# A hybrid RG-LRU and mLSTM decoder step: when the rows of w_out are loaded, the order of the mLSTM output products, and the load of W

## The chip, the cores and the metric

One core of one Trainium2 chip runs the whole program. Its engines are TensorE (PE; PEld is its weight load), VectorE (DVE), ScalarE (ACT), GpSimd (POOL) and SyncE (SP), which here only issues DMAs; GpSimd issues DMAs too. The metric is the device time of one execution in microseconds. Lower is better.

## The reference

One layer of a decoder runs on a prompt of 1,024 tokens and, apart from it, on eight decode tokens that bring their own state. The core of what must be computed:

```python
hn = rmsnorm(x, g_norm)
u = hn @ w_in                                  # 1024 -> 7 x 1024 + 8 columns
xa, za, uq, uk, uv, uo, zb, ui, uf = split(u)
yA, hA, bufA = rglru_branch(xa, ...)           # causal conv, two gates, linear scan
hB, C, n, m = mlstm_seq(q, k, v, ig, lf, ...)  # 4 heads of 256, chunks of 128 tokens
yB = sigmoid(uo) * hB
yB = yB * rsqrt(mean(yB * yB, per head) + EPS) * g_mhead
merged = concat([yA * silu(za), yB * silu(zb)])   # 2048 wide
x = x + merged @ w_out                            # (2048, 1024)
y = rmsnorm(x, g_final)
```

Within a chunk, with `w = exp(D - m_t)` the masked decay weights, each head computes

```python
P = w * einsum('bthk,bshk->bhts', q, k)
num = einsum('bhts,bshv->bthv', P, v) + ginter * einsum('bthk,bhkv->bthv', q, C)
C_new = carry_scale * C + einsum('bhs,bshk,bshv->bhkv', decay, k, v)
```

The program returns y for prompt and decode tokens and the states of both branches.

## The kernel before

The large products are made from operands split into a high and a low part: `split` copies the value into a rounded type on ScalarE, and VectorE subtracts to get the rest; `mm3` then adds three products (high x high, high x low, low x high; lines 64 to 66).

**The input projection** walks over 14 units (`UNITS`) of two 256-column blocks of `w_in`. Each unit takes seven products, `Q_P1` to `Q_P4`, whose left operands (`cb_hi`, `cb_lo`, one pair for each of the seven) are made once from the normalised prompt and lie in 14 slots `b0` to `b13` of the pool `bpool`: `cb_hi` of product q in slot 2q, `cb_lo` in slot 2q+1. The last unit is the last reader of these slots, so product by product they become free there. The other operands, `wh` and `wl`, are split two products ahead into the pool `ws`, six slots of 4 KB a partition, from two raw tiles (`raw0`, `raw1`, 8 KB a partition each).

Between the halves of the products, `pop_bg` emits background work from queues: gates, RG-LRU, decode, the first chunk of the mLSTM (`m_first`), and, in the last unit, rows 0 to 7 of `w_out`.

**w_out** has 16 row blocks of 128 x 1024. `wo_load(n)` asks for rows n and n+1, each into a `ws` slot (`oraw`, line 1180). `wo_prep(n)` multiplies both with the decode tokens' merged activations (line 1194; `mAd` for rows 0 to 7, `mBd` for 8 to 15, both 32 columns wide with eight in use; the sums stay in the PSUM bank `tr` over all 16 rows) and splits them: rows 0 to 7 plainly into slot m, rows 8 to 15 with the head gain `gm4` multiplied in (lines 1203 and 1204), rows 14 and 15 into the raw slots. `wo_due(q)`, called after product q of the last unit, queues `wo_prep(0)`, `(2)`, `(4)`, `(6)` and, after the last product, the load of the first RG-LRU rows (`o_load(0)`). Rows 8 to 11 are prepared before the chunk loop, 12 and 13 in item 4, 14 and 15 in item 5.

**The chunk loop** runs over items n = 4 to 31: chunk c = n // 4, head h = n % 4. For each item `m_a` makes scores and weights, `m_b` the output and the new state, `m_g` and `m_z` gate, normalise and transpose the output into `mh`, `ml`. `m_load(n + 2)` fetches W, q and k, and v two items ahead. W is the row of decay exponents, broadcast to 128 partitions (three buffers); `m_k` adds a bias and the mask on VectorE (line 1038), takes the exponential on ScalarE (line 1039), and `m_a` multiplies the scores with it (line 1067).

Between these steps `fill` emits pieces of the output projection, two row blocks each, from the generators in `work`. `out_part(c, half, part)` makes one half (512 columns) of one tile of 128 tokens; part 0 uses the eight RG-LRU row blocks, part 1 the eight mLSTM row blocks, both into one PSUM tile (`o`, three banks). After part 1 the tile is added to x on VectorE (line 1275), squared on ScalarE (line 1276), and after both halves normalised by `finish`. A chunk's share of `work` is: part 0 of half 0 of tile c, part 1 of both halves of tile c-1, part 0 of half 1 of tile c. The last tile is made apart by `last_part` and `last_tile`.

What decides the order: the code gives the instructions in program order with symbolic buffers, and a planner in the build orders each engine's queue ahead of time. It takes, at each moment of its own model of the run, the earliest instruction in program order that is ready by that model; so an instruction that is ready early can stand far ahead of its place in the code, and a load can stand as early as its buffer is free. On the chip each queue runs strictly in that order.

## Time and profile before

| | |
|---|---|
| Median of 3 runs | 966.44 us (966.21 to 969.55) |
| The profiled execution | 970.22 us, of which span 968.1 us |
| Mean granted TensorE clock | 0.993 |
| TensorE busy | 941.3 us (97%) |
| VectorE, ScalarE, GpSimd busy | 697.4, 546.1, 146.5 us |
| Moved by DMA | 153.17 MB, mean 158 GB/s |

The busy time of an engine in a window says whether it is full there; the clock beside it says how fast TensorE was allowed to run. Successive large matmuls start 0.23 us apart and are listed with 0.39 us each, since they overlap; so short waits can hide in a "busy" TensorE, and the starts are what counts. In timelines, the bracket behind an instruction is the idle time of its engine just before it, and what ended it. "issue" of a DMA is the instruction on the queue; the landing is seen in the wait of who uses the data.

### The profile page before, as it was taken

What the parts mean: (1) busy time and instruction counts of PE and PEld (TensorE: products, weight loads), DVE (VectorE), ACT (ScalarE), POOL (GpSimd) and SP (SyncE); (2) the same over time, 40 slices, a digit from 0 to 9 for tenths busy, and PEclk for the clock granted to TensorE, in tenths of its full rate; (3) what the DMA queues carried; (4) which work ended last, traced back from release to release, by engine and by line L of the source; (5) the groups of instructions that cost most, each with busy time, mean ns of one, the idle gap of its engine ahead of it and who ended that gap; (6) DMA issues with size and microseconds to landing.
All of it is one profiled execution on the core that took longest, in us unless ns stands there. A gap on an engine that the chain in (4) does not pass through costs nothing.

```text
span 968.1 us, 15367 instructions
## 1 busy us (share of the span) xinstructions
PE 941.3 (97%) x5402; PEld 768.4 (79%) x5402; DVE 697.4 (72%) x1447; ACT 546.1 (56%) x984; POOL 146.5 (15%) x260
## 2 busy tenths in 40 slices
PE   7999989999999999899999999999999999999997
PEld 7797767777787988687889898875667788888886
DVE  6775898988888877777786846686566677676764
ACT  6554456666666756454566744456546366465643
POOL 1111112121212122202212221010200100000020
PEclk9999999999999999999999999999999999999999
DMA  5431447356645455437645453424973754564481
GB/s 191 137 126 43 131 134 271 129 176 196 220 152 196 166 177 172 156 124 242 193 163 167 150 180 95 157 93 154 308 212 98 197 142 128 150 184 140 120 110 49
DMA packets 129314, 153.17 MB, mean 158 GB/s; under 512 B 13750, under 2 KB 107990, under 8 KB 129230
## 3 DMA queue, kind: packets, MB, share of 16 engines
q1 hardware_dynamic: 111510, 96.33, 33.8%
q0 software_dynamic: 17728, 55.87, 16.7%
q8 instruction: 42, 0.69, 0.3%
q14 instruction: 34, 0.28, 0.1%
HBM read 100.59 MB, written 51.65 MB: 157 GB/s over the span
## 4 chain that ended last, share of the span: by engine, by line
PE 43%; DMA 5%; DVE 5%; issue 4%; ACT 1%; POOL 0%; SPq 0%; DVEq 0%; POOLq 0%; ACTq 0%
PE ps_o L66 7%; PE ps_o L64 7%; PE ps_o L65 7%; PE ps_kv L64 5%; PE ps_kv L65 5%; PE ps_kv L66 5%; DMA W<-d_alpha 3%; PE ps_tr L227 1%; PE ps_s L1058 1%; DVE Cl L71 1%; PE ps_qp L64 1%; DVE Cf L1119 1%; DMA rh<-d_rm 1%; PE ps_qp L65 1%; PE ps_qp L66 1%
## 5 line engine op out<-in xcount | busy, mean ns | idle before, releaser
L70 ACT CAST wh<-raw 128x1024 fp32r<-128x1024 f32 x91 | 95.5, 1050 | 74.7 <-PE ps_o L65 24.5
L71 DVE TENSOR_TENSOR wl<-raw,wh 128x1024 fp32r<-128x1024 f32 x91 | 110.9, 1218 | 31.6 <-ACT wh L70 19.4
L64 PE MATMUL ps_kv<-cb_hi,wh 128*128 128x512 f32 x320 | 129.0, 403 | 0.1
L66 PE MATMUL ps_kv<-cb_hi,wl 128*128 128x512 f32 x320 | 126.1, 394 | 0.0
L65 PE MATMUL ps_kv<-cb_lo,wh 128*128 128x512 f32 x320 | 125.9, 393 | 0.0
L64 PE MATMUL ps_o<-cb_hi,wh 128*128 128x512 f32 x240 | 94.7, 394 | 0.0
L66 PE MATMUL ps_o<-cb_hi,wl 128*128 128x512 f32 x240 | 93.9, 391 | 0.0
L65 PE MATMUL ps_o<-cb_lo,wh 128*128 128x512 f32 x240 | 93.7, 390 | 0.0
L64 PEld LDWEIGHTS ps_kv<-cb_hi,wh 128*128 128x128 f32 x320 | 60.4, 189 | 24.8 <-issue 5.5
L66 PEld LDWEIGHTS ps_kv<-cb_hi,wl 128*128 128x128 f32 x320 | 60.5, 189 | 15.7 <-issue 2.5
L65 PEld LDWEIGHTS ps_kv<-cb_lo,wh 128*128 128x128 f32 x320 | 60.6, 189 | 11.9
L66 PE MATMUL ps_o<-wo,ml 128*128 128x512 f32 (+1 forms) x136 | 52.2, 384 | 3.2 <-DVE ml L71 3.1
L64 PE MATMUL ps_kv<-wh,cb_hi 128*128 128x256 f32 x192 | 55.3, 288 | 0.0
L65 PE MATMUL ps_kv<-wl,cb_hi 128*128 128x256 f32 x192 | 54.3, 283 | 0.0
L66 PE MATMUL ps_kv<-wh,cb_lo 128*128 128x256 f32 x192 | 54.3, 283 | 0.0
L64 PE MATMUL ps_o<-wo,rh 128*128 128x512 f32 (+1 forms) x136 | 53.9, 397 | 0.0
L64 PEld LDWEIGHTS ps_o<-cb_hi,wh 128*128 128x128 f32 x240 | 45.1, 188 | 10.8 <-issue 1.7
L66 PEld LDWEIGHTS ps_o<-cb_hi,wl 128*128 128x128 f32 x240 | 45.0, 188 | 10.3 <-issue 0.8
L64 PE MATMUL ps_o<-wo,mh 128*128 128x512 f32 (+1 forms) x136 | 52.9, 389 | 0.0
L65 PE MATMUL ps_o<-wo,rh 128*128 128x512 f32 (+1 forms) x136 | 52.3, 384 | 0.0
L65 PEld LDWEIGHTS ps_o<-cb_lo,wh 128*128 128x128 f32 x240 | 45.1, 188 | 9.0
L66 PE MATMUL ps_o<-wo,rl 128*128 128x512 f32 (+1 forms) x136 | 52.1, 383 | 0.0
(469 smaller groups left out, 2506.9 us busy)
## 6 DMA issues: line engine op xcount, KB each, us to landing
raw<-in_w_in_dram SPq DMA_DIRECT2D x56, 512.0 KB
Cb<-in_state_mlstm_C_dram SPq DMA_DIRECT2D x32, 256.0 KB
out_dram<-Cb POOLq DMA_DIRECT2D x32, 256.0 KB, 4.6
qk<-d_qk SPq DMA_DIRECT2D x32, 256.0 KB
oraw<-in_w_out_dram SPq DMA_DIRECT2D x16, 512.0 KB
d_qk<-s POOLq DMA_DIRECT2D x24, 256.0 KB, 4.2
x<-in_x_prompt_dram SPq DMA_DIRECT2D x8, 512.0 KB
d_x<-s POOLq DMA_DIRECT2D x16, 256.0 KB, 2.9
```

Source lines behind the costliest of these rows:

```text
L64: TE.matmul(out, ah, bh, start=first, stop=False, skip_group_check=True)
L65: TE.matmul(out, ah, bl, start=False, stop=False, skip_group_check=True)
L66: TE.matmul(out, al, bh, start=False, stop=last, skip_group_check=True)
L70: A.copy(hi, src)
L71: V.tensor_tensor(lo, src, hi.bitcast(F32), op=ALU.subtract)
L227: TE.matmul(pz[32 * g:32 * g + 32, :], hnd[:, k, :], raws[u, k // 4][:, k % 4, :], start=k < 4, stop=k >= 4, skip_group_check=True)
L1058: TE.matmul(S, qk[:, 2 + kb, :], qk[:, kb, :], start=kb == 0, stop=kb == 1)
L1119: V.scalar_tensor_tensor(mx["Cf"][h][:, kb, :], mx["Cf"][h][:, kb, :], cs_b[:, h, c:c + 1], kvs[kb], op0=ALU.mult, op1=ALU.add)
```

## The change

Three parts, and small ones with them.

1. `wo_load` puts rows 0 to 7 as pairs into one operand slot, `b1`, rows 8 and 9 into `raw0`, rows 10 and 11 into `raw1`, and only rows 12 to 15 into `ws` slots. The split rows go to other slots (`WO_SLOT`): row 0 to `b0`, rows 1 to 12 to `b2` to `b13`, row 13 to `b1`. `wo_load` is called ahead of `wo_prep`, which now splits a single row and, for an even row, first issues the decode products of the pair (`wo_dec`). In the last unit rows 0 to 11 are due instead of 0 to 7; rows 12 and 13 come before the chunk loop, 14 in item 4, 15 in item 5. `o_load(0)` is called after the fifth product instead of the seventh.
2. Part 1 of a tile is one generator, `out_m(c)`: the first pair of heads (row blocks 8 to 11) for both halves, then the second pair (12 to 15) for both halves. Part 0 is `out_r(c, half)`. The order in `work` stays.
3. W has four buffers, and `m_load(n)` calls `w_load(n + 1)`: q, k and v are asked for two items ahead as before, W three.

With them: the decode weights are 32 columns wide for rows 0 and 1 only (`mA0`), which write all 32 rows of each sum once, and eight columns wide for all others, so the clearing of `mBd` on GpSimd goes, and one VectorE step in `rg_final` becomes two.

```diff
-    mAd = const([P, 8, 32], "mAd")
+    mA0, mA1 = const([P, 2, 32], "mA0"), const([P, 6, NB], "mA1")
...
-        V.scalar_tensor_tensor(mAd[:, :, 0:NB], OC[:, :, 4:12], 0.5, na, op0=ALU.mult, op1=ALU.mult)
+        for d, s in ((mA0[:, :, 0:NB], slice(0, 2)), (mA1, slice(2, 8))):
+            V.scalar_tensor_tensor(d, OC[:, s, 4:12], 0.5, na[:, s], op0=ALU.mult, op1=ALU.mult)
...
-        mB.append(sg([P, 8, 32], "mBd"))
+        mB.append(sg([P, 8, NB], "mBd"))
         mBd = mB[0]
-        G.memset(mBd, 0.0)
...
+        w_load(0)
         m_load(0)
         m_load(1)
...
-        W = mx["p"].tile([P, L], F32, tag="W", name="W", bufs=3)
-        ld(W, d_alpha[h:h + 1, ts_].rearrange("o t -> (o t)").partition_broadcast(P))
+        w_load(n + 1)
...
+    def w_load(n):
+        if n < 4 * NCH:
+            c, h = n // 4, n % 4
+            Ws[n] = mx["p"].tile([P, L], F32, tag="W", name="W", bufs=4)
+            ld(Ws[n], d_alpha[h:h + 1, c * L:(c + 1) * L].rearrange("o t -> (o t)").partition_broadcast(P))
...
+    WO_SLOT = [0, 2, 3, 4, 5, 6, 7, 8, 9, 10, 11, 12, 13, 1, 14, 15]
+
+    def wo_buf(slot, name, dt=F32R):
+        return big(slot, [P, 2, T], name, dt) if slot < 14 else rawp.tile([P, 2, T], dt, tag=f"raw{slot - 14}", name=name)
+
     def wo_load(n):
 
-        for m in (n, n + 1):
-            oraw[m] = ws([P, T], f"oraw{m}", F32)
-            ld(oraw[m], w_out[0, m * P:(m + 1) * P, :])
-
-    def wo_prep(n):
+        if n < 12:
+            t = wo_buf({8: 14, 10: 15}.get(n, 1), f"oraw{n}", F32)
+            rows = [t[:, 0], t[:, 1]]
+        else:
+            rows = [ws([P, T], f"oraw{n + i}", F32) for i in range(2)]
+        for i, r in enumerate(rows):
+            ld(r, w_out[0, (n + i) * P:(n + i + 1) * P, :])
+            oraw[n + i] = r
+
+    def wo_dec(n):
...
+                TE.matmul(dec_o[0][32 * g:32 * g + (32 if n == 0 else NB), :], md, oraw[m][:, half * 512:(half + 1) * 512],
+                          start=n == 0, stop=n == 14, skip_group_check=True)
+
+    def wo_prep(m):
+
+        if m % 2 == 0:
+            wo_dec(m)
+        raw = oraw.pop(m)
+        t = wo[m] = wo_buf(WO_SLOT[m], f"wo{m}")
+        if m < 8:
+            split(t[:, 0], t[:, 1], raw)
+        else:
+            gm = gm4[:, m - 8:m - 7]
+            A.mul(t[:, 0], raw, gm)
+            V.scalar_tensor_tensor(t[:, 1], raw, gm, t[:, 0].bitcast(F32), op0=ALU.mult, op1=ALU.subtract)
...
+    def out_m(c):
+
+        x = ot[c]
+        for pair in range(2):
+            for half in range(2):
+                yield from out_mm(x, half, (ch[c]["mh"], ch[c]["ml"]), 1, range(4 * pair, 4 * pair + 4))
+                if pair == 0:
+                    continue
...
+                V.tensor_tensor(x["y"][half], x["y"][half], x["p", half], op=ALU.add)
+                A.activation(x["p", half], x["y"][half], AF.Square, accum_out=x["ms"][:, half:half + 1])
...
     def wo_due(q):
 
+        if q > 0:
+            wo_prep(2 * q - 1)
         if q < 4:
+            wo_load(2 * q)
+        if q == 4:
+            wo_load(8)
+            wo_load(10)
+            o_load(0)
+        if q == 5:
+            wo_load(12)
+        if q < 6:
             bg.append(lambda: wo_prep(2 * q))
-        if q == 6:
-            bg.append(lambda: o_load(0))
...
-    work.extend([out_part(0, 0, 0), out_part(0, 1, 0), out_part(1, 0, 0), out_part(0, 0, 1), out_part(0, 1, 1),
-                 out_part(1, 1, 0)])
+    work.extend([out_r(0, 0), out_r(0, 1), out_r(1, 0), out_m(0), out_r(1, 1)])
     m_k(4)
-    wo_load(8)
+    wo_prep(12)
+    wo_load(14)
     fill(2)
-    wo_load(10)
-    wo_prep(8)
+    wo_prep(13)
     fill(2)
-    wo_load(12)
-    wo_prep(10)
...
             if c == 1:
-                wo_prep(12)
-                wo_load(14)
+                wo_prep(14)
                 o_load(1)
...
             if c == 1:
-                wo_prep(14)
+                wo_prep(15)
```

More of the change, by code (lines that the diff above doesn't have):

```diff
@@ L141, in hymba_kernel @@
     dEM = dconst([P, NB, NH], "dEM")
-    mAd = const([P, 8, 32], "mAd")
+    mA0, mA1 = const([P, 2, 32], "mA0"), const([P, 6, NB], "mA1")
     hnd = dconst([P, KC, 32], "hnd")
-    for t in (mAd, hnd):
+    for t in (mA0, hnd):
         G.memset(t, 0.0)
@@ L960, in decode_outputs @@
         for kb in range(2):
-            V.tensor_tensor(v4(mBd[:, :, 0:NB], kb), v4(num, kb), rsq, op=ALU.mult)
+            V.tensor_tensor(v4(mBd, kb), v4(num, kb), rsq, op=ALU.mult)
         yield
@@ L1015, in m_load @@
         ld(vt, d_v[h][ts_, :])
-        it[n] = {"qk": qk, "vt": vt, "W": W}
+        it[n] = {"qk": qk, "vt": vt}
+    Ws = {}
+    def w_load(n):
[3 more added lines that the diff above has]
+            ld(Ws[n], d_alpha[h:h + 1, c * L:(c + 1) * L].rearrange("o t -> (o t)").partition_broadcast(P))
     sos = {}
@@ L1036, in m_k @@
         d = it[n]
-        W = d["W"]
+        W = d["W"] = Ws.pop(n)
         V.scalar_tensor_tensor(W, W, be_t[:, c, h:h + 1], maskT, op0=ALU.add, op1=ALU.min)
@@ L1168, in m_z @@
         split(x["mh"][:, s, :], x["ml"][:, s, :], z)
-    wo = []
+    wo = {}
     dec_o = []
     oraw = {}
+    WO_SLOT = [0, 2, 3, 4, 5, 6, 7, 8, 9, 10, 11, 12, 13, 1, 14, 15]
+    def wo_buf(slot, name, dt=F32R):
+        return big(slot, [P, 2, T], name, dt) if slot < 14 else rawp.tile([P, 2, T], dt, tag=f"raw{slot - 14}", name=name)
     def wo_load(n):
-        for m in (n, n + 1):
-            oraw[m] = ws([P, T], f"oraw{m}", F32)
-            ld(oraw[m], w_out[0, m * P:(m + 1) * P, :])
@@ L1182, in wo_prep @@
-    def wo_prep(n):
+        if n < 12:
[7 more added lines that the diff above has]
+    def wo_dec(n):
         if n == 0:
             dec_o.append(ps("tr", [P, 512]))
-        if n not in oraw:
-            wo_load(n)
@@ L1189, in wo_prep @@
         for i in range(2):
             m = n + i
-            md = mAd[:, m, :] if m < 8 else mB[0][:, m - 8, :]
+            md = mA0[:, m, :] if m < 2 else mA1[:, m - 2, :] if m < 8 else mB[0][:, m - 8, :]
             for half in range(2):
                 g = 2 * i + half
-                TE.matmul(dec_o[0][32 * g:32 * g + 32, :], md, oraw[m][:, half * 512:(half + 1) * 512], start=n == 0,
-                          stop=n == 14, skip_group_check=True)
-        for m in (n, n + 1):
-            raw = oraw.pop(m)
-            t = big(m, [P, 2, T], f"wo{m}") if m < 14 else rawp.tile([P, 2, T], F32R, tag=f"raw{m - 14}", name=f"wo{m}")
-            if m < 8:
-                split(t[:, 0], t[:, 1], raw)
-            else:
-                gm = gm4[:, m - 8:m - 7]
-                A.mul(t[:, 0], raw, gm)
-                V.scalar_tensor_tensor(t[:, 1], raw, gm, t[:, 0].bitcast(F32), op0=ALU.mult, op1=ALU.subtract)
-            wo.append(t)
+                TE.matmul(dec_o[0][32 * g:32 * g + (32 if n == 0 else NB), :], md, oraw[m][:, half * 512:(half + 1) * 512],
+                          start=n == 0, stop=n == 14, skip_group_check=True)
@@ L1255, in o_load, with out_r, out_mm @@
         ot[c] = {"r": (mh, ml)}
-    def out_part(c, half, part):
+    def out_r(c, half):
         x = ot[c]
-        if part == 0:
-            x["p", half] = ps("o", [P, 512])
-        mh, ml = x["r"] if part == 0 else (ch[c]["mh"], ch[c]["ml"])
+        x["p", half] = ps("o", [P, 512])
+        yield from out_mm(x, half, x["r"], 0, range(8))
+    def out_mm(x, half, mhl, part, ks):
+        mh, ml = mhl
         hs = slice(half * HT, (half + 1) * HT)
-        for k in range(8):
+        for k in ks:
             w = wo[8 * part + k]
@@ L1268, in out_part @@
                 yield
-        if part == 1:
-            if half == 0:
-                x["ms"] = fms()
-                x["y"] = [sg([P, HT], f"y{n}") for n in range(2)]
-                for n in range(2):
-                    stq(x["y"][n], x_prompt[0, c * P:(c + 1) * P, n * HT:(n + 1) * HT])
-            V.tensor_tensor(x["y"][half], x["y"][half], x["p", half], op=ALU.add)
-            A.activation(x["p", half], x["y"][half], AF.Square, accum_out=x["ms"][:, half:half + 1])
-            if half == 1:
-                finish(P, x["y"], x["ms"], y_p[0, c * P:(c + 1) * P, :], True)
-                del ot[c], ch[c]
+    def out_m(c):
[5 more added lines that the diff above has]
+                    continue
+                if half == 0:
+                    x["ms"] = fms()
+                    x["y"] = [sg([P, HT], f"y{n}") for n in range(2)]
+                    for n in range(2):
+                        stq(x["y"][n], x_prompt[0, c * P:(c + 1) * P, n * HT:(n + 1) * HT])
+                V.tensor_tensor(x["y"][half], x["y"][half], x["p", half], op=ALU.add)
+                A.activation(x["p", half], x["y"][half], AF.Square, accum_out=x["ms"][:, half:half + 1])
+        finish(P, x["y"], x["ms"], y_p[0, c * P:(c + 1) * P, :], True)
+        del ot[c], ch[c]
     LP = [slice(0, 512), slice(512, 768), slice(768, 1024)]
@@ L1418, in hymba_kernel @@
         if h == 0 and c > 1:
-            work.extend([out_part(c, 0, 0), out_part(c - 1, 0, 1), out_part(c - 1, 1, 1)])
-            work.append(out_part(c, 1, 0) if c < last else last_part(0))
+            work.extend([out_r(c, 0), out_m(c - 1), out_r(c, 1) if c < last else last_part(0)])
         m_a(n)
```

## The prediction

> **What bounds the kernel now.** I read the page first, then the busy time by stage, then TensorE's waits, then the timelines around the places where TensorE stands still.

> ```profile
> span 968.1 us, 15367 instructions
> ## 1 busy us (share of the span) xinstructions
> PE 941.3 (97%) x5402; PEld 768.4 (79%) x5402; DVE 697.4 (72%) x1447; ACT 546.1 (56%) x984; POOL 146.5 (15%) x260
> ```

> TensorE is busy for 97% of the span, and the change takes no product away. It can win only where TensorE idles, runs at a lower clock, or issues small matmuls badly. By stage (the last two rows are parts of the second):

> ```profile
> core 0: us, PE busy (x) PEld busy (x) DVE busy (x) ACT busy (x) POOL busy (x), PEclk, DMA share, GB/s
> 640.00:690.00 50.00, 49.83 (x217) 33.30 (x216) 33.38 (x65) 26.31 (x35) 5.09 (x11) 1.00 0.53 173
> 690.00:725.00 35.00, 32.87 (x163) 21.90 (x162) 22.21 (x40) 17.69 (x32) 3.54 (x7) 0.95 0.77 247
> 725.00:770.00 45.00, 43.15 (x236) 34.81 (x235) 29.23 (x92) 23.05 (x63) 4.87 (x9) 1.00 0.52 150
> 700.00:710.00 10.00, 8.18 (x44) 5.82 (x43) 6.32 (x11) 5.84 (x10) 0.00 (x0) 0.94 1.03 317
> 710.00:720.00 10.00, 10.00 (x49) 6.54 (x47) 6.06 (x16) 4.32 (x11) 0.55 (x1) 0.89 0.36 105
> ```

> 640 to 690 is the last unit of the input projection, with the first eight rows of w_out between its products; 690 to 725 is the passage to the chunk loop, with the other eight. The unit is full. The passage idles 2.1 us, has the lower clock, and there the DMA engines are full (1.03). What stands still in it, on TensorE, ScalarE and the load queue:

> ```profile
> 706.02 0.39 PE L66 MATMUL ps_o<-wo,rl 128*128 128x512 f32 x1
> 708.23 0.39 PE L64 MATMUL ps_qp<-vh,ph 128*128 128x258 f32 x1 [1.82 <-ACT hh L1114]
> ...
> 700.08 0.93 SPq L1180 DMA_DIRECT2D oraw<-in_w_out_dram  x2
> ...
> 705.83 1.15 ACT L1203 ACTIVATE wo<-oraw,gm 128x1024 fp32r<-128x1024 f32 x1 [3.52 <-DMA oraw<-in_w_out_dram]
> ...
> 707.71 0.47 ACT L1114 ACTIVATE hh<-ps_qp,gi_t 128x257 f32<-128x257 f32 x1
> ```

> The chain: row 14 is requested at 700.08 and lands at 705.83. ScalarE stands in front of its split for 3.52 us, with the evacuation `hh` behind it in the same queue; the next product of item 4 writes the same PSUM bank (`qp`, because the decode sums hold `tr`) and waits for `hh`: 1.82 us. Right after that the clock falls.

> **The change, part by part.** The sum is against the profiled execution: 970.2 us, of which 968.1 span; that is 3.8 us above the median 966.4 of the runs, so I carry the difference to the median.

> *Rows ahead of their splits.* Sixteen loads of 512 KB before and after. Rows 0 to 7 now land in operand slot 1, a pair at a time, from the end of the unit's first product on; rows 8 to 11 in the two raw slots, which free once the last operands are split; rows 12 to 15 in the `ws` pool. Thus four rows are loaded, summed for decode and split some 10 to 20 us earlier, and the passage keeps four rows instead of eight. Their splits cost this much:

> ```profile
> L1203 ACT ACTIVATE wo<-oraw,gm x8: 1137/1150/1153, 689.5 to 708.1; 128x1024 fp32r<-128x1024 f32 x8
> L1204 DVE SCALAR_TENSOR_TENSOR wo<-oraw,gm,wo x8: 1278/1284/1285, 690.7 to 713.3; 128x1024 fp32r<-128x1024 f32 x8
> ```

> Four rows are 4 x 1.15 = 4.6 us of ScalarE and 4 x 1.28 = 5.1 us of VectorE, moved into 640 to 690, where they are busy 26.3 and 33.4 of 50 us. That is hidden, as long as neither stands long before a late row.

> The stall goes: -1.8. ScalarE's 3.52 us before row 14 came from a load that took 5.8 us on full DMA engines. With rows 8 to 11 out of the way it is issued when the last operands free, near 690, and its decode batch stands at 711.5 now.

> The low clock goes with it. The rows 700:710 and 710:720 lack 0.06 and 0.11 of 10 us: 0.6 + 1.1 = 1.7 us. [...]

> The decode sums. Each row of w_out is multiplied with the eight decode tokens, four matmul records a row. In these windows (line 1194 alone) a batch costs TensorE about the same whether it is one row or two:

> ```profile
> 655.50:657.00 1.50, 1.05 (x4) 0.14 (x4) 1.00 0.04 11
> 691.00:692.40 1.40, 1.05 (x4) 0.14 (x4) 1.00 0.95 369
> 692.50:694.00 1.50, 1.05 (x4) 0.14 (x4) 1.00 1.07 423
> 696.00:699.00 3.00, 1.54 (x8) 0.29 (x8) 1.00 0.97 387
> 702.50:704.50 2.00, 1.07 (x8) 0.16 (x8) 1.00 1.08 346
> 711.50:713.50 2.00, 1.04 (x2) 0.14 (x2) 0.85 0.37 112
> 715.50:717.50 2.00, 1.06 (x6) 0.15 (x6) 1.00 0.05 13
> ```

> Rows 8 to 15 cost 1.05 + 1.05 + 1.54 + 1.07 + 1.04 + 1.06 = 6.8 us. If both rows of a pair have landed, a batch of eight costs 1.07, and four of them 4.3: -2.5. If rows 8 to 11 still come one by one it is 4 x 1.05 + 2 x 1.07 = 6.3: -0.5. I take the middle, -1.5. Rows 0 to 7 stay single: each pair is requested only when slot 1 frees, so the rows arrive one behind the other as now (0 there; -4.1 if all four pairs joined, 8 x 1.05 - 4 x 1.07, which the serial slot excludes). Eight columns of weights in place of 32: the loads hide beside the matmuls (0.14 us a batch); 0, or -1 for all.

> New waits. Of two rows issued together the first lands 3.9 us later (next fence), and each pair of rows 2 to 7 goes through slot 1: request, landing, ScalarE's and VectorE's split, release. The decode matmuls stand in TensorE's order, so a late row stops TensorE.

> ```profile
> 649.96 0.81 SPq L1180 DMA_DIRECT2D oraw<-in_w_out_dram  x2
> ...
> 653.83 1.04 ACT L70 CAST wo<-oraw 128x1024 fp32r<-128x1024 f32 x1 [0.67 <-DMA oraw<-in_w_out_dram]
> ...
> 679.41 1.05 ACT L70 CAST wo<-oraw 128x1024 fp32r<-128x1024 f32 x1 [2.62 <-DMA oraw<-in_w_out_dram]
> ...
>   PEld ps_tr L1194: 2.2, 4
> ...
>   PE ps_tr L1194: 0.3, 1
> ```

> Now TensorE waits 0.3 us for rows in all (its weight loads 2.2, mostly covered), ScalarE up to 2.62 at once in this unit. Ends: -0.3 (even that wait goes) and +7.9 (three pairs by 2.62). I take +0.7, nearest to the present rows. Behind a blocked load on SP's queue stand item 5's q and k and the first RG-LRU rows, wanted only from about 688 on.

> *Products by pairs of heads.* The same 48 matmuls a chunk. The second pair's operands gain half an item; no wait names them, the wait for `ml` being at a tile's first product, which needs the first pair in both orders. Half 0 now ends later, and its PSUM tile is wanted by `out_r(c, 1)`: there are three `o` banks, and all three are taken.

> ```profile
> 769.03 0.68 DVE L1275 TENSOR_TENSOR y<-y,ps_o 128x512 f32<-128x512 f32 x1
> ...
> 770.33 0.19 ACT L1276 ACTIVATION_READ_ACCUMULATOR ps_o<-y 128x1 f32 x1
> ...
> 772.70 0.40 PE L66 MATMUL ps_o<-wo,ml 128*128 128x512 f32 x1
> 772.93 0.28 PE L64 MATMUL ps_qp<-Ch,qh 128*128 128x258 f32 x1
> ...
> 774.71 0.40 PE L64 MATMUL ps_o<-wo,mh 128*128 128x512 f32 x1
> ```

> An evacuation takes 770.52 - 769.03 = 1.5 us. Between half 0's last product and `out_r(c, 1)` lie 12 products at 0.23 (2.8) and item work of 774.71 - 772.93 = 1.8: 4.6 us of cover. With VectorE blocked for 4.3 us in between (next part) it would need 5.8, so 1.2 us over, times six chunks: ends 0 and +7; I take 0, since VectorE's block comes in another item than the evacuation mostly.

> *W three items ahead.*

> ```profile
> L1011 SPq DMA_DIRECT2D W<-d_alpha x32: 319/382/485, 566.6 to 912.5; - x32
> L1038 DVE SCALAR_TENSOR_TENSOR W<-W,be_t,maskT x32: 340/352/354, 573.0 to 915.5; 128x128 f32<-128x128 f32 x32
> ...
> L1067 DVE SCALAR_TENSOR_TENSOR pf<-ps_s,W x32: 278/284/293, 579.2 to 936.6; 128x128 f32<-128x128 f32 x32
> ...
> 752.02 0.32 SPq L1011 DMA_DIRECT2D W<-d_alpha  x1
> ...
> 758.80 0.35 DVE L1038 SCALAR_TENSOR_TENSOR W<-W,be_t,maskT 128x128 f32<-128x128 f32 x1 [4.30 <-DMA W<-d_alpha]
> ...
> 761.15 0.50 PE L66 MATMUL ps_o<-wo,ml 128*128 128x512 f32 x1 [1.85 <-DVE ml L71]
> ...
> PE ps_o L66 <- DVE ml L71: 3.1, 3, 1.8
> ```

> VectorE's W step makes TensorE wait: 4.30 us before it, then 1.85 on `ml`. But the step is not urgent: the last load is at 912.5, its step at 915.5, 3.0 us behind, and the product that uses it (line 1067) at 936.6, 21 us later. The order of instructions puts each step right behind its load, whenever a slot frees. A fourth slot lets the load and the step both move one item further; VectorE still meets W a few us after its request. I take 0; ends -3.1 (all the waits for `ml` go) and +1.

> *The rest.* One memset less on GpSimd, one small VectorE step more in `rg_final`: 0, both beside full products.

> Sum: -1.8 - 1.7 - 0.3 - 1.5 + 1.0 (the new waits of 0.7 beside the 0.3 of the old) = -4.3 us: 970.2 becomes 965.9, and against the median 966.4 - 4.3 = **962.1**, 0.45% less. About 0.5% (4.8 us) is what a measurement of this kernel can tell from no change.

> **The rivals.**
> *Slower: slot 1 is a chain that TensorE waits for.* A pair needs 5.7 us to land (653.83 for the first row, the second's batch at 655.7) and 2.3 to be split, 8.0 in all; a product of the unit takes about 7. For: the chain is the longer, and more loads share the DMA engines than now. Against: it starts one pair ahead. Price: three pairs by 2.62 = 7.9, and a clock loss of 1.7 behind it, in place of the 0.7 taken: 962.1 + 8.9 = 971.0. From 5.0 us of such waits on, the change loses.
> *W's waits go.* -3.1 more: 959.0. For: it is what TensorE waits for in the chunks; against: the hoisted steps.
> *The passage's stall stays.* `hh` stands behind some other late row (14 or 15, now both asked for at once when `ws` slots free): 1.8 + 1.7 are not won: 965.6.
> *The low clock comes back behind another wait.* 1.82 us brought it at 708, 1.85 us at 761 did not (1.00 in the row 725:770). If timing shifts so that the other one meets it, 1.7 come back: 963.8. [...]

> **How the numbers follow.** Forecast 0.40 (its own range 959.5 to 964.5), slot chain 0.20, W 0.16, stall stays 0.14, clock 0.10. Below 961.6: some 0.45 of the forecast and nearly all of W: 0.34. Above 971.3: half of the chain, and 0.06 for the pairs' 7 us and for what a new order of all instructions may do: 0.16. The rest, 0.50, is within 0.5%. The range goes from below W's case to just over the chain's, 957 to 971.5.

> **What would show it.** Right: no wait of `ps_qp` on `hh` near 706, 1.00 clock in the passage, batches x8 on line 1194 for rows 8 to 15, x4 for rows 0 to 7; VectorE's waits for W still tens of us and those for `ml` still there. Wrong: TensorE or its weight loads waiting for `oraw` by microseconds between 650 and 690; waits of `ps_o` on `y`'s evacuation at line 64; or W steps without a wait before them.

## The result, and the profile after

| | before | after |
|---|---|---|
| Median of 5 runs | 967.14 us (966.21 to 969.55) | 976.71 us (972.52 to 978.16) |
| Ratio to before | | 1.0086, 95% interval 1.0057 to 1.0114 |
| The profiled execution | 970.22 us, span 968.1 | 978.16 us, span 976.2 |

The changed kernel is 0.9% slower. The forecast was 962.1 us, its range ended at 971.5. In the code after, the W load is line 1024, the W step 1046, the exponential 1047, the weighting `pf` 1075, the row load 1198, the decode products 1211 and the splits of rows 8 and up 1224 and 1225; the evacuation `hh` is line 1122 on ScalarE and 1129 on VectorE.

From the page after, the span and the busy times:

```profile
span 976.2 us, 15359 instructions
PE 941.8 (96%) x5402; PEld 771.5 (79%) x5402; DVE 700.0 (72%) x1448; ACT 543.1 (56%) x982; POOL 146.0 (15%) x259
```

TensorE does the same products in nearly the same busy time, so the 8.1 us of span are waiting and clock. Of them 0.6 us arise ahead of the last unit: the last raw operands are asked for at 620.39 us before and at 620.95 after. The busy time by stage, after, in the columns of before:

```profile
core 0: us, PE busy (x) PEld busy (x) DVE busy (x) ACT busy (x) POOL busy (x), PEclk, DMA share, GB/s
640.00:690.00 50.00, 44.88 (x190) 29.05 (x189) 34.77 (x65) 25.32 (x32) 3.81 (x7) 0.97 0.58 194
690.00:725.00 35.00, 30.46 (x160) 21.34 (x159) 16.40 (x26) 14.37 (x26) 4.87 (x9) 0.95 0.57 181
725.00:770.00 45.00, 42.12 (x219) 33.50 (x217) 27.53 (x85) 22.16 (x60) 3.78 (x7) 0.96 0.46 133
```

The last unit, full before (49.83 of 50), idles 5.1 us and starts to lose clock. The clock lost is 50 x 0.03 + 35 x 0.05 + 45 x 0.04 = 5.05 us; before it was 1.7. TensorE's waits after, and VectorE's for W (us in total, how many times, the longest):

```profile
PE ps_tr L1211 <- DMA oraw<-in_w_out_dram: 4.9, 3, 2.9
PE ps_qp L64 <- ACT hh L1122: 4.5, 1, 4.5
PE ps_qp L1172 <- DVE hh L1129: 2.4, 1, 2.4
PE ps_o L66 <- DVE ml L71: 1.7, 2, 1.0
...
DVE W L1046 <- DMA W<-d_alpha: 40.7, 21, 6.2
```

The same rows of before, where the second wait on `hh` does not occur:

```profile
PE ps_qp L64 <- ACT hh L1114: 1.8, 1, 1.8
PE ps_tr L1194 <- DMA oraw<-in_w_out_dram: 0.3, 1, 0.3
...
DVE W L1038 <- DMA W<-d_alpha: 42.1, 23, 4.3
```

So the balance of the two profiled executions, after less before: waits for rows 4.9 - 0.3 = +4.6; waits on `hh` 4.5 + 2.4 - 1.8 = +5.1; on `ml` 1.7 - 3.1 = -1.4; clock 5.05 - 1.7 = +3.4; decode batches -2.9 (below). That is +8.8, where 8.1 were measured; TensorE's other waits change by about -0.3 in all.

**The long wait.** After's chain, in order of time (start, length, what; "DMA" runs from request to landing), and TensorE and its neighbours in the timeline:

```profile
702.30 6.14 DMA d_zs<-c
708.58 0.36 SPq L1038
...
709.04 0.53 SPq L1013
...
709.62 4.76 DMA W<-d_alpha
...
721.64 5.48 DMA W<-d_alpha
```

```profile
704.65 2.71 DVE L1225 SCALAR_TENSOR_TENSOR wo<-oraw,gm,wo 128x1024 fp32r<-128x1024 f32 x2 [2.65 <-ACT wo L1224]
707.28 0.28 DVE L1075 SCALAR_TENSOR_TENSOR pf<-ps_s,W 128x128 f32<-128x128 f32 x1
...
714.41 0.35 DVE L1046 SCALAR_TENSOR_TENSOR W<-W,be_t,maskT 128x128 f32<-128x128 f32 x1 [6.18 <-DMA W<-d_alpha]
714.80 0.31 ACT L1047 ACTIVATE W<-W 128x128 f32<-128x128 f32 x1 [6.90 <-DVE W L1046]
...
716.84 0.58 PE L64 MATMUL ps_qp<-vh,ph 128*128 128x258 f32 x1 [4.52 <-ACT hh L1122]
```

Read it from the end. TensorE stands until 716.84 for `hh` of item 4. In ScalarE's queue, this `hh` stands behind the exponential of W(8), the W of item 8. In VectorE's queue, the W step of item 8 stands right behind item 4's weights, and both engines stand still for it (6.18 and 6.90 us). Item 8 is four items away: no one needs this W yet. It had only just been asked for (709.62). Its slot comes free with `pf` of item 4, which ended at 707.56 because the splits of the last rows stood in front of it. Then the load of `z` and that of q and k went first on SP's queue, and `z` waited until 708.58 for the store of the last gate block, which was issued at 702.30.

The second wait is the same thing one item on: the W of item 9 is asked for at 721.64 and takes 5.5 us. VectorE stands for it with `hh` of item 5, here VectorE's own, further back in its queue:

```profile
727.15 0.35 DVE L1046 SCALAR_TENSOR_TENSOR W<-W,be_t,maskT 128x128 f32<-128x128 f32 x1 [2.96 <-DMA W<-d_alpha]
...
730.23 1.11 PE L1172 MATMUL ps_qp<-idF,hh 128*128 128x128 f32 x4 [2.41 <-DVE hh L1129]
```

**The rows.** TensorE's timeline in the last unit after, and the first split on ScalarE with SP's timeline (the row of 656.91 from a narrower window):

```profile
664.11 1.03 PE L1211 MATMUL ps_tr<-oraw,mA 128*8 128x512 f32 x4 [2.89 <-DMA oraw<-in_w_out_dram]
666.33 1.88 PE L1211 MATMUL ps_tr<-oraw,mA 128*8 128x512 f32 x4 [0.22 <-DMA oraw<-in_w_out_dram]
...
688.70 1.03 PE L1211 MATMUL ps_tr<-oraw,mA 128*8 128x512 f32 x4 [1.74 <-DMA oraw<-in_w_out_dram]
...
693.61 1.04 PE L1211 MATMUL ps_tr<-oraw,mBd 128*8 128x512 f32 x8
697.53 1.04 PE L1211 MATMUL ps_tr<-oraw,mBd 128*8 128x512 f32 x8
708.96 1.04 PE L1211 MATMUL ps_tr<-oraw,mBd 128*8 128x512 f32 x8
```

```profile
648.58 1.04 ACT L70 CAST wo<-oraw 128x1024 fp32r<-128x1024 f32 x1 [2.22 <-DMA oraw<-in_w_out_dram]
...
644.82 13.37 SPq L1198 DMA_DIRECT2D oraw<-in_w_out_dram  x6
...
656.91 1.28 SPq L1198 DMA_DIRECT2D oraw<-in_w_out_dram  x3
...
668.68 6.85 SPq L1198 DMA_DIRECT2D oraw<-in_w_out_dram  x4
...
682.28 15.94 SPq L1198 DMA_DIRECT2D oraw<-in_w_out_dram  x6
```

Row 2 landed 7.2 us after its request at 656.91, when rows 3, 8 and 9 were on their way too; the first row of the first pair, alone with its partner, took 3.8 us (644.82 to 648.58). Row 3's batch takes 1.88 us in place of 1.03, since it runs at half clock behind the wait for row 2. Rows 10 to 15 came as three batches of eight at 1.04 us each, and rows 8 and 9 one right behind the other with row 7. All decode products together keep TensorE busy for 13.14 us (640 to 716) where it was 15.23 before (640 to 720). Without the 0.85 us that the half clock adds to row 3's batch, which the balance has under clock, that is -2.9: the upper case of the prediction (-2.5) and a little more.

### The profile page after: what moved, and what is told of

Same layout as the page of the kernel before. It is cut to its first block, busy times and chain, and to the rows that moved or that the text cites. A ratio compares the mean times of both kernels' runs of the same rounds, so it can differ in the third digit from the quotient of the medians.

```text
span 976.2 us, 15359 instructions
## 1 busy us (share of the span) xinstructions
PE 941.8 (96%) x5402; PEld 771.5 (79%) x5402; DVE 700.0 (72%) x1448; ACT 543.1 (56%) x982; POOL 146.0 (15%) x259
## 3 DMA queue, kind: packets, MB, share of 16 engines
q1 hardware_dynamic: 111510, 96.33, 33.4%
## 4 chain that ended last, share of the span: by engine, by line
PE 34%; issue 11%; DMA 6%; DVE 5%; POOL 1%; ACT 1%; SPq 0%; POOLq 0%; ACTq 0%; DVEq 0%
PE ps_o L66 6%; PE ps_o L64 6%; PE ps_o L65 6%; DMA W<-d_alpha 5%; PE ps_kv L64 4%; PE ps_kv L66 3%; PE ps_kv L65 3%; PE ps_s L1066 1%; DVE Cf L1127 1%; POOL d_zs L345 1%; PE ps_tr L227 1%; DVE Cl L71 1%; DMA d_zs<-c 1%; DMA rh<-d_rm 1%; PE ps_qp L64 1%
## 5 line engine op out<-in xcount | busy, mean ns | idle before, releaser
L70 ACT CAST wh<-raw 128x1024 fp32r<-128x1024 f32 x91 | 95.6, 1050 | 74.6 <-PE ps_o L65 26.9
L71 DVE TENSOR_TENSOR wl<-raw,wh 128x1024 fp32r<-128x1024 f32 x91 | 111.1, 1221 | 32.1 <-ACT wh L70 19.9
L64 PE MATMUL ps_kv<-cb_hi,wh 128*128 128x512 f32 x320 | 129.1, 404 | 0.0
L66 PE MATMUL ps_kv<-cb_hi,wl 128*128 128x512 f32 x320 | 126.4, 395 | 0.0
L64 PE MATMUL ps_o<-cb_hi,wh 128*128 128x512 f32 x240 | 94.5, 394 | 0.0
L66 PE MATMUL ps_o<-cb_hi,wl 128*128 128x512 f32 x240 | 93.9, 391 | 0.0
L64 PEld LDWEIGHTS ps_kv<-cb_hi,wh 128*128 128x128 f32 x320 | 60.5, 189 | 23.9 <-issue 5.5
L66 PEld LDWEIGHTS ps_kv<-cb_hi,wl 128*128 128x128 f32 x320 | 60.5, 189 | 15.6 <-issue 2.6
L64 PE MATMUL ps_kv<-wh,cb_hi 128*128 128x256 f32 x192 | 55.2, 288 | 0.0
L66 PE MATMUL ps_kv<-wh,cb_lo 128*128 128x256 f32 x192 | 54.3, 283 | 0.0
L66 PEld LDWEIGHTS ps_o<-cb_hi,wl 128*128 128x128 f32 x240 | 45.1, 188 | 11.1 <-issue 1.7
L66 PE MATMUL ps_o<-wo,ml 128*128 128x512 f32 (+1 forms) x136 | 52.1, 383 | 1.7 <-DVE ml L71 1.7
L64 PE MATMUL ps_o<-wo,rh 128*128 128x512 f32 (+1 forms) x136 | 53.6, 394 | 0.0
L64 PE MATMUL ps_o<-wo,mh 128*128 128x512 f32 (+1 forms) x136 | 53.0, 390 | 0.0
L64 PEld LDWEIGHTS ps_o<-cb_hi,wh 128*128 128x128 f32 x240 | 45.1, 188 | 9.9 <-issue 0.8
L66 PE MATMUL ps_o<-wo,rl 128*128 128x512 f32 (+1 forms) x136 | 52.1, 383 | 0.0
```

The source lines that it names most:

```text
L64: TE.matmul(out, ah, bh, start=first, stop=False, skip_group_check=True)
L66: TE.matmul(out, al, bh, start=False, stop=last, skip_group_check=True)
L70: A.copy(hi, src)
L71: V.tensor_tensor(lo, src, hi.bitcast(F32), op=ALU.subtract)
```

## The experiments

Each edit is against the kernel named. All of them compute everything. Kernels that ran together share the runs of the kernel before, and each ratio is to these: to a median of 967.74 us for `e_rows`, `e_pairs`, `e_w` and `e_after_hold`, 967.36 for `e_before_hold`, `e_rows_hold`, `e_hold_late8` and `e_hold_ws`, and 966.86 for `e_after_hold2`, `e_late8` and `e_rows_hold_late8`. Where two kernels of different groups are compared, it is by their ratios.

**First: one part of the change at a time.** `e_rows` has the new schedule of the rows and the narrow decode weights, with three W buffers and the order by halves as before. `e_pairs` has only the order by pairs of heads. `e_w` has only W three items ahead; the narrow weights go along, since they make the room for the fourth buffer. Their edits are the corresponding parts of the diff above:

```diff
 # e_rows: the changed kernel, with
-        w_load(n + 1)
+        W = mx["p"].tile([P, L], F32, tag="W", name="W", bufs=3)
+        ld(W, d_alpha[h:h + 1, ts_].rearrange("o t -> (o t)").partition_broadcast(P))
...
-            work.extend([out_r(c, 0), out_m(c - 1), out_r(c, 1) if c < last else last_part(0)])
+            work.extend([out_part(c, 0, 0), out_part(c - 1, 0, 1), out_part(c - 1, 1, 1)])
...
```

> The kernel before with the new row schedule alone: rows of w_out in slot b1, the raw slots and ws, single-row splits, decode weights of eight columns; products by halves and three W buffers as before. If the row schedule makes the loss, this stands 5 to 10 us above the kernel before (972 to 977), with TensorE waiting 3 us or more for rows of w_out (line 1211 in the changed kernel) in the last unit. If the loss came from W's fourth buffer or from the pairs, it is within 2 us of the kernel before.

> The kernel before with the mLSTM output products by pairs of heads alone. The prediction took 0 with ends 0 and +7: 965 to 969, and no wait of TensorE for an o bank. If the pairs share in the loss, 2 us or more above the kernel before, with waits of ps_o for the evacuation of y.

> The kernel before with four W buffers and W asked for one item earlier, and the eight-column decode weights that make room for the buffer. The prediction took 0: within 2 us of the kernel before, VectorE's waits for W still 35 to 45 us in total, since its W step is only put one item further ahead. If the earlier load had worked, those waits fall below 15 us and the time by up to 3 us. If the extra lead itself harms, as W steps land in front of the passage's work, 2 to 5 us slower.

Measured: `e_rows` 972.22 us, ratio 1.0051 (1.0029 to 1.0073); `e_pairs` 967.86 us, 1.0000 (0.9972 to 1.0027); `e_w` 963.99 us, 0.9971 (0.9948 to 0.9994). TensorE's waits in `e_rows`:

```profile
PE ps_qp L64 <- ACT hh L1114: 4.9, 1, 4.9
PE ps_tr L1203 <- DMA oraw<-in_w_out_dram: 2.9, 3, 1.7
...
PE ps_qp L1164 <- DVE hh L1121: 2.3, 1, 2.3
```

The schedule of the rows alone brings both waits on `hh`, with three buffers for W as with four, and again VectorE stands at the W step in front of the first (6.97 us). So the greater part of the loss belongs to the rows, and the fourth buffer neither makes the two waits nor cures them. The late rows that the expectation named are there too (2.9 us), but they are the smaller part. Alone, W three ahead gains 0.29%, some 2.8 us, more than the 2 us of the expectation, although VectorE still waits for W for 40.1 us in 22 places as expected. Its profile has 1.4 us of waits for `ml` instead of 3.1, and its wait on `hh` (2.2 us, behind a late row as before) had no half clock behind it; the narrow weights have a share that no run separates. The parts hardly add: +0.51, 0.00 and -0.29% make +0.2%, and all together are +0.86%, a difference just beyond the intervals.

**Second: the W step held back.** An order edge, no wait, puts the W step of item n behind `pf` of item n - 1 on VectorE; the load stays where it was.

```diff
-        V.scalar_tensor_tensor(W, W, be_t[:, c, h:h + 1], maskT, op0=ALU.add, op1=ALU.min)
+        step = V.scalar_tensor_tensor(W, W, be_t[:, c, h:h + 1], maskT, op0=ALU.add, op1=ALU.min)
+        if n - 1 in pfs:
+            tc.add_manual_dep(step.ins, pfs[n - 1].ins.name, mybir.DependencyInfo(
+                mybir.DependencyClass.NoSync, mybir.DependencyReason.DATA), reason="W step behind pf")
...
-        V.scalar_tensor_tensor(pf, S, 1.0 / 16.0, d["W"], op0=ALU.mult, op1=ALU.mult)
+        pfs[n] = V.scalar_tensor_tensor(pf, S, 1.0 / 16.0, d["W"], op0=ALU.mult, op1=ALU.mult)
```

`e_after_hold` is this on the changed kernel, `e_before_hold` on the kernel before, `e_rows_hold` on `e_rows`.

> The changed kernel, with one order edge more: the W step of item n stands behind the weights (pf) of item n-1 on VectorE, so it can no longer be put in front of the queue two or three items ahead, right behind its load. Theory: the waits of 4.5 and 2.4 us in the passage are VectorE standing at the W step, and the two half-clock stretches behind them cost 1.7 us each; they go, and VectorE's waits for W fall below 5 us in all: 8 to 10 us less than the changed kernel, 967 to 969, with the waits for rows in the last unit (4.9 us) still there. Rival: the passage waits for something else that is late, and W only stands in front of it: 974 or more, with the same waits under another name.

> The kernel before, with the W step of item n behind the weights of item n-1 and nothing else. Theory: in the kernel before, W's step costs TensorE only the waits for ml, 3 us; its wait for hh near 706 comes from row 14 on ScalarE and stays, with the half clock behind it: 3 to 4 us faster, 963 to 965. Rival: the held step alone makes the whole gain of the changed kernel with it, and the rows none: 961 or less, and no wait for hh.

> The new row schedule with the held W step, products by halves and three W buffers. If the pairs and the fourth buffer are worth nothing, it is within 2 us of the changed kernel with the held step (960.8), and the waits for hh of the row schedule alone (4.9 and 2.3 us) are gone. If the fourth buffer is what makes the held step free, W waits come back and it is 964 or more.

Measured: `e_after_hold` 960.83 us, ratio 0.9931 (0.9902 to 0.9960); `e_before_hold` 962.83 us, 0.9958 (0.9935 to 0.9981); `e_rows_hold` 958.56 us, 0.9897 (0.9863 to 0.9930). By ratios the edge takes 1.0086 - 0.9931 = 1.55% (15 us) from the changed kernel, more than the 8 to 10 us expected, 1.0051 - 0.9897 = 1.54% from `e_rows`, and 0.42% (4 us) from the kernel before, about what was expected. In `e_after_hold` and `e_rows_hold` neither a wait of VectorE for W nor one of TensorE on `hh` is listed any more. TensorE's waits on `hh`, `ml` and rows in `e_before_hold`, the whole of them:

```profile
PE ps_qp L64 <- ACT hh L1119: 2.0, 1, 2.0
PE ps_tr L1199 <- DMA oraw<-in_w_out_dram: 0.5, 1, 0.5
```

and in `e_rows_hold`:

```profile
PE ps_tr L1208 <- DMA oraw<-in_w_out_dram: 2.4, 2, 1.3
```

This pair shows the two causes apart. On the kernel before, the edge takes the waits for `ml` (3.1 us) and leaves the wait on `hh`, which stands behind a late row (ScalarE waits 2.94 us for it); in this profile no half clock follows. With the new schedule beside the edge that wait is gone too: -4.3 us by the medians of these two, -0.6% by their ratios, with some 0.4% to either side. That the medians give the -4.3 us of the prediction is luck in part, since the terms are others: no half clock was there to be won, and the waits for rows grew by 1.9 us. So the new schedule is a gain where nothing else takes the place of the wait that it removes. `e_rows_hold` and `e_after_hold` differ by the pairs and the fourth buffer; with the step held, these two bring nothing that the runs can tell.

**Third: two edges alone.** The same edge on the changed kernel, on the steps of items 8 and 9 alone, of 32.

```diff
-        if n - 1 in pfs:
+        if n in (8, 9):
```

> The changed kernel, with the order edge on two of its 32 W steps alone: those of items 8 and 9, the two in front of which VectorE stood still in the passage (6.18 us at 714.41, 2.96 us at 727.15). Theory: these two alone make TensorE's waits on hh (4.5 and 2.4 us) and the two stretches of half clock behind them (1.7 us each), so this kernel is some 8 to 11 us under the changed one: 966 to 969. The rest of what the edge on all steps brought, some 5 to 8 us, must then come from the loop. Rival: the edge on all steps helped because the whole order of the loop came out otherwise; then two edges bring under 4 us, 973 or more, and a wait on hh is still there.

Measured: 961.56 us, ratio 0.9947 (0.9923 to 0.9971); by ratios 1.39% or 13 us under the changed kernel, where 8 to 11 were expected. The passage and the stage behind it, and what is left of the waits:

```profile
690.00:725.00 35.00, 35.00 (x191) 26.68 (x190) 20.56 (x45) 15.78 (x34) 3.52 (x7) 1.00 0.71 210
725.00:770.00 45.00, 45.00 (x252) 38.05 (x252) 30.67 (x95) 27.09 (x71) 4.87 (x9) 1.00 0.47 143
```

```profile
DVE W L1048 <- DMA W<-d_alpha: 30.7, 21, 3.4
...
PE ps_tr L1216 <- DMA oraw<-in_w_out_dram: 2.8, 2, 1.6
...
PE ps_o L66 <- DVE ml L71: 0.9, 3, 0.4
```

Both stages are full and at full clock: the waits on `hh` are gone (6.9 us), and the two stretches of half clock behind them (3.4). That is 10.3 us, within what was expected, and it was two instructions of 15,359 by their place in a queue: TensorE's order is the same in both kernels, and up to the first of these two steps so is that of every other queue; behind it the small steps of the decode output stand in another order too. VectorE still waits 30.7 us for W, nearly all of it in the loop, and that costs TensorE too little for these runs to tell: the edge on all steps has the ratio 0.9931, on two 0.9947. TensorE's longest wait behind the passage is now one of 1.62 us at 780.14 for the normalisation of `m_n`, where after has one of 0.97. The 5 to 8 us that the expectation left to the loop are not there.

The profile of this kernel has 2.1 us less of row waits than after's and no half clock behind row 2. This lies ahead of the first edge, where the queues are alike, so it is a difference of two executions and not of the kernels: the same rows cost 4.9, 2.8 and 2.1 us in the profiles of the changed kernel, of this one and of `e_after_hold`. The 13 us of the ratios have an interval of their own: with 0.28 and 0.24% on the two ratios, some 3.5 us to either side.

**Fourth: the rows in flight.** Rows 8 and 9 are asked for behind row 5, rows 10 and 11 behind row 7, again by an order edge alone.

```diff
-            ld(r, w_out[0, (n + i) * P:(n + i + 1) * P, :])
+            rowld[n + i] = ld(r, w_out[0, (n + i) * P:(n + i + 1) * P, :])
+            if n in (8, 10):
+                tc.add_manual_dep(rowld[n + i].ins, rowld[n - 3].ins.name, mybir.DependencyInfo(
+                    mybir.DependencyClass.NoSync, mybir.DependencyReason.DATA), reason="row load behind another")
```

`e_late8` is this on the changed kernel, `e_hold_late8` on `e_after_hold`, `e_rows_hold_late8` on `e_rows_hold`. `e_hold_ws` is `e_after_hold` with rows 0 to 7 in `ws` slots as before, so without the chain through slot 1:

```diff
-        if n < 12:
-            t = wo_buf({8: 14, 10: 15}.get(n, 1), f"oraw{n}", F32)
+        if n in (8, 10):
+            t = wo_buf({8: 14, 10: 15}[n], f"oraw{n}", F32)
```

> The changed kernel, with the loads of rows 8 and 9 ordered behind that of row 5 on SP's queue, and those of 10 and 11 behind row 7's; the W steps are left as they are. Theory: the late rows 2, 3 and 6 come from four rows in flight together, so the waits for rows fall from 4.9 us to under 1 and the half clock behind the first goes: some 5 us less, 970 to 973, while the two waits on hh in the passage stay. Rival: the rows' waits come from the chain through slot 1 itself, then they stay within 2 us of 4.9, and the time within 2 us of the changed kernel's.

> The changed kernel with the held W step, and the loads of rows 8 and 9 behind row 5's, of 10 and 11 behind row 7's. If rows 2 and 3 come late because rows 8 and 9 share the DMA engines with them, TensorE's wait for row 2 (1.6 to 2.9 us) falls below 0.5 and the time by 1 to 2 us. If they come late because their load cannot start before slot b1 is released, the waits stay and the time is within 1 us of 960.8.

> The changed kernel with the held W step, and rows 0 to 7 loaded into ws slots as before, not through slot b1; rows 8 to 11 still ahead in the raw slots. If the pairs' chain through one slot costs what TensorE waits for rows there (2 us, and a half-clock stretch of 1.7 in some executions), it is 2 to 3 us faster than 960.8. Rival: the ws slots it takes hold back the last operands, and the time is the same or worse.

> The kernel before with the new row schedule, the held W step and the late loads of rows 8 to 11; three W buffers and the order by halves as before. If the two gains add (the late loads gave 4.6 us beside four buffers, and three buffers with the order by halves stood at 958.6 with the held step): 954 to 956, the fastest of all. If the late loads' gain was a matter of how waits and clock windows met in that one kernel: 957 to 960.

Measured: `e_late8` 967.27 us, ratio 1.0006 (0.9976 to 1.0036); `e_hold_late8` 956.20 us, 0.9875 (0.9833 to 0.9917); `e_hold_ws` 958.29 us, 0.9890 (0.9858 to 0.9922); `e_rows_hold_late8` 957.38 us, 0.9887 (0.9850 to 0.9924). TensorE's waits for rows: 1.0 us in `e_late8`, where the five profiles with both the chain through slot 1 and rows 8 to 11 asked for early had 2.1 to 4.9; 0.4 us in `e_hold_late8`, 0.2 in `e_rows_hold_late8`, 0.8 in `e_hold_ws`. The chain through slot 1 is still there in `e_late8`, so the chain by itself did not make rows 2, 3 and 6 late. In `e_hold_ws` the chain is gone and rows 8 to 11 are still asked for early, and the wait is small too. So it took both: rows asked for just in time, and other rows on the DMA engines beside them.

`e_late8` is 0.8% or 7.7 us under the changed kernel by ratios, with some 4 us to either side, where 5 were expected. The two waits on `hh` were expected to stay, since the W step keeps its place in the queue. The second does (2.3 us, with its half clock), but the first is down to 0.82. The order of TensorE's instructions from the last unit's end through the passage is the same in both kernels. In `e_late8`:

```profile
693.46 2.64 DVE L1229 SCALAR_TENSOR_TENSOR wo<-oraw,gm,wo 128x1024 fp32r<-128x1024 f32 x2 [1.69 <-ACT wo L1228]
696.02 0.28 DVE L1075 SCALAR_TENSOR_TENSOR pf<-ps_s,W 128x128 f32<-128x128 f32 x1
...
696.34 0.49 SPq L1024 DMA_DIRECT2D W<-d_alpha  x1
...
701.06 0.35 DVE L1046 SCALAR_TENSOR_TENSOR W<-W,be_t,maskT 128x128 f32<-128x128 f32 x1 [4.09 <-DMA W<-d_alpha]
...
703.00 0.39 PE L64 MATMUL ps_qp<-vh,ph 128*128 128x258 f32 x1 [0.82 <-ACT hh L1122]
```

W takes as long to land (4.7 us here, 4.8 after). But it is asked for 0.04 us behind `pf`, where after has 2.06 (707.56 to 709.62), and the splits in front of `pf` come earlier: from the request to the place where TensorE begins to wait lie 703.00 - 0.82 - 696.34 = 5.8 us, after 716.84 - 4.52 - 709.62 = 2.7. These 3.1 us are most of the 3.7 us (4.52 - 0.82) by which the wait is shorter. So, as far as one profile of each shows, the rows' lateness and the W step are one chain: late rows make late splits, these a late `pf` and a late last gate block, these a late request of W, and the step in its place in the queue hands all of it to TensorE. Either end can be cut; holding the step cuts more (15 us against 7.7).

Lowest of all is `e_hold_late8`, 1.25% under the kernel before (0.83 to 1.67%); by medians it gained 4.6 us on `e_after_hold`, where 1 to 2 were expected, but by ratios the gain is 0.56% with some 0.5% to either side. `e_rows_hold`, `e_hold_ws` and `e_rows_hold_late8` lie within its interval: on `e_rows_hold` the late loads brought nothing that can be told (0.9887 against 0.9897), so the two gains did not add. `e_hold_ws` gained 2.5 us on `e_after_hold` by medians, as expected, but its ratio (0.9890 against 0.9931) is within the intervals too. These four kernels have four to six runs each; which of them is the fastest stays open.

## Why the prediction was wrong

The order of the steps is that of the prediction.

*The stall goes, -1.8, and the low clock with it, -1.7.* This is the step that failed: the path to `hh` had a second late load in it. That row 14 made the stall of before was right: `e_before_hold`, with all of W's waits gone, still has it (2.0 us), and it goes when the rows are rescheduled (`e_rows_hold`). What was not asked is what would be late next in ScalarE's queue in front of `hh`. It was W: its exponential in front of `hh` on ScalarE, then its step in front of `hh` on VectorE. That made waits of 4.5 + 2.4 us and two stretches of half clock, 6.9 + 3.4 = 10.3 us, where the 3.5 us of before were to vanish. `e_after_hold2` shows it: with these two steps alone held back, both waits and both stretches are gone. The rival "the passage's stall stays" had the kind of thing, another late load in front of `hh`, but looked for a row and priced it as the stall of before. The prediction quoted the loads of W of 4.3 us in front of VectorE and said that they were not urgent, which is right and was the reason to fear them: a step that nobody needs can stand anywhere, and the order put it right behind its load everywhere, also in the passage.

*W three items ahead, 0.* Right in what was said: "the load and the step both move one item further; VectorE still meets W a few us after its request", 40.7 us in 21 places beside 42.1 in 23. Alone (`e_w`) it is -0.29% or -2.8 us, inside the ends given (-3.1 to +1) but not the 0 that was taken. What the term lacked was that its 0 held for the chunk loop, where the products of item 4 and its neighbours are covered. In the passage the cover is TensorE's work between the request and `hh`, only 2.7 us in the changed kernel.

*SP's queue.* The prediction named item 5's q and k and the RG-LRU rows behind a blocked load, and not W behind the load of `z`, which waits for the last gate block's store. That is the 2 us between `pf` and the request, of the wait of 4.5.

*New waits, +0.7.* Mis-sized: 2.1 to 4.9 us in the five profiles with this schedule (2.9 in `e_rows`, 2.4 in `e_rows_hold`), inside the ends given (-0.3 to +7.9), and in the profile after 1.7 of clock behind row 2. The slot's period was taken as 8.0 us; pairs were asked for at 644.82, 656.91, 668.68 and 682.28, 12 to 13.6 us apart, and row 2 took 7.2 us to land. The rival of the slot chain foresaw the wait, but the chain alone does not make it (`e_late8`, 1.0 us): it takes rows 8 and 9 in flight beside it, which the rival named only as "more loads share the DMA engines than now", without a price.

*Decode sums, -1.5.* Better than taken: -2.9, a little past the upper case, with three batches of eight at 1.04 us and rows 8 and 9 beside row 7.

*Pairs of heads, 0.* Right (`e_pairs`, 1.0000), and no wait on the evacuation of `y` appeared.

*The low clock behind another wait.* As a rival it was worth 1.7 us; in fact three waits had a stretch of half clock behind them instead of one, 3.4 us more. That of two like waits before, 1.82 and 1.85 us, one had it and the other not was read rightly (last section).

The sum of the terms was -4.3. With the terms as the profiles have them it would be +5.1 (waits on `hh`) + 4.6 (rows) + 3.4 (clock) - 2.9 (decode) - 1.4 (`ml`) = +8.8; by the ratio of the runs the change is +0.86%, 8.3 us. The rows' 4.6 is the highest of five profiles, so its size in this sum is partly chance.

## What to carry to other kernels

Before a wait is costed away, list what else stands in front of the waiting instruction in the queues that release it, and look in particular for steps that nobody needs yet: here an instruction that waited for a fresh load stood in front of everything behind it in its queue (VectorE 6.18 us for the W of item 8, and TensorE 4.52 us for the `hh` behind it), and its own slack was no protection. A planner that sets each instruction as early as its model allows can put such steps right behind their loads. Here an order edge without any wait, on two instructions, turned a loss of 0.9% into a gain of 0.5%. Loads brought forward competed with loads that were already just in time (row 2 took 7.2 us to land beside rows 3, 8 and 9, where the first row of the first pair took 3.8; TensorE's waits for rows were 4.9 us after and 1.0 in `e_late8`): price their landing with all that is in flight, not from a row of a load that was alone.

## What the runs showed of the hardware

A half-speed stretch of TensorE's clock followed some waits of about 2 us and not others. By the rows of waits and windows at their places: 1.82 us before (with), 2.2 in `e_pairs` (with), 2.3 in `e_rows` (with), 2.4 after (with), 2.3 in `e_late8` (with); 1.85 before (without), 2.2 in `e_w` (without), 2.0 in `e_before_hold` (without). The waits of 2.89 and 4.52 us after and of 4.9 in `e_rows` all had one. The three stretches of after begin at 665.31, 716.51 and 730.17 us. Each lasts 3.41 us at a granted clock of 0.50 and so loses 1.7 us of clock, behind waits of 2.89, 4.52 and 2.41 us alike.

```profile
705.29:708.70 3.41, 1.59 (x11) 1.13 (x10) 1.68 (x3) 2.87 (x5) 0.00 (x0) 1.00 1.03 321
708.70:712.11 3.41, 3.41 (x13) 2.59 (x11) 2.08 (x6) 1.28 (x3) 0.00 (x0) 0.50 0.49 118
759.90:763.31 3.41, 2.16 (x9) 1.80 (x10) 3.41 (x9) 0.75 (x2) 1.11 (x2) 1.00 0.30 79
```

```profile
702.17:705.59 3.42, 2.32 (x16) 1.86 (x15) 0.13 (x1) 1.31 (x2) 0.00 (x0) 1.00 0.85 324
705.59:709.00 3.41, 1.99 (x12) 1.62 (x12) 3.41 (x7) 2.61 (x6) 0.00 (x0) 1.00 0.93 257
```

Before, the wait of 1.82 us lies whole in one window (3.41 - 1.59 = 1.82), and the next window has half the clock. The wait of 1.85 us lies in two: the window shown has 3.41 - 2.16 = 1.25 us idle, and the clock stays at 1.00. The wait of 2.2 us in `e_w` is spread over the two shown, which have 1.1 and 1.4 us idle, and the clock stays at 1.00 from 700 to 730 us. From 100 us on and without the last 8 us, the traces of before and after have six windows with 1.82 to 3.41 us idle, each with one at half clock behind it (at 398.09 and 705.29 before; at 399.07, 661.90, 713.10 and 726.75 after); the one with the most idle time among all others, 1.74 us at 685.79 after, has none. In the first 35 us, half clock also followed windows with 1.05 us (before) and 1.50 and 0.89 us (after) idle, and did not follow two of before with 1.45 and 1.49; that stays unexplained. What sets the clock these runs do not show.

Profiled executions of one order differ before the change touches anything. The last loads of raw operands ahead of the last unit are issued at 620.95 us after and at 618.00 in `e_after_hold2`, whose queues are the same up to there, and the granted clock of the first 100 us is 0.97 in the one and 1.00 in the other: after has two half-clock stretches there, the other none. Before, 31 runs lie between 961.82 and 973.21 us. That is why sizes here are taken from ratios over many runs, and from stages of a profile, not from the spans of two profiles.
